# Second block's attention: scores and products on all 128 rows, q projected earlier, the output product in two halves of four blocks

## The chip, the cores and the metric

One core of a Trainium2 chip (trn2). The time is the device time of one execution of the whole program in microseconds; a kernel's time is the median of its runs.

## The reference

The program is two small models one after the other; the second one's layers are the diff attention (da), a gated FFN with a short convolution, the top-k sparse attention (dsa), and a second FFN. All of it is float32, with 528 tokens (16 meta tokens and 512 others) of width 1024. What the change touches is this:

```python
def diff_attention(h, w_qkv, lq1, lk1, lq2, lk2, subln, w_o, cos, sin, lambda_init):
    q, k, v = jnp.split(h @ w_qkv, 3, axis=-1)
    q = apply_rope(q.reshape(B, T, 8, 2, 64), cos, sin) * (64 ** -0.5)
    k = apply_rope(k.reshape(B, T, 8, 2, 64), cos, sin)
    v = v.reshape(B, T, 8, 128)
    lam = exp(sum(lq1 * lk1)) - exp(sum(lq2 * lk2)) + lambda_init
    s = einsum('bqhcd,bkhcd->bhcqk', q, k)            # two score maps per head pair
    p = softmax(where(k_pos <= q_pos, s, -inf))
    a = p[:, :, 0] - lam * p[:, :, 1]
    o = rms_norm(einsum('bhqk,bkhe->bqhe', a, v), subln) * (1.0 - lambda_init)
    return o.reshape(B, T, 1024) @ w_o

def dsa_attention(h, w_in, idx_k_norm, w_o, cos, sin, n_keys):
    q, k, v, qi, ki, wi = jnp.split(h @ w_in, DSA_SPLITS, axis=-1)   # 16 heads of 64, 8 index heads
    score = einsum('bqhk,bqh->bqk', relu(qi . ki) / 8, wi * 8 ** -0.5)
    score = where(causal, where(k_pos < 16, 1e30, score), -inf)
    keep the top min(256, n_keys // 4) keys of each query; softmax and product with v over these alone
    return o.reshape(B, T, 1024) @ w_o
```

The sliding-window attention (swa) of the first model has scores of 128 queries against 256 keys, and a first block that has only its own 128 keys.

## The kernel before, in words

Activations stand transposed in SBUF: 8 tiles of 128 features by 528 tokens. Every large product goes through `gemm` (line 366): each float32 operand is split into a high and a low part of type fp32r, and three products (high by high, high by low, low by high) of a 128x128 block are summed in PSUM, in pieces of 256, 258, 272 or 512 columns. Weights come from HBM in 294 chunks of 512 KB; ACT makes the high part (line 320) and DVE the low one (line 322). A scheduler sets the order of each engine's list at build time and interleaves the next product with the attention that is being worked on; the engines then run their lists in order and wait for one another on semaphores.

Both attentions go over eight pairs of heads. For each pair q and k are projected (`rope`, lines 770 to 774: a copy on ACT, a shuffle and products on DVE, one product on POOL, line 773, and a last sum on DVE, line 774). The queries are cut into five tiles: 16 meta tokens (i = 0) and four of 128 (i = 1 to 4); tile i reads the keys up to its own end (16, 144, 272, 400, 528).

- **Scores.** `pair_scores` picks one of two forms. `scores` (line 973), for i = 0 and 1, multiplies plain float32 q and k on the 64 rows of a head; PE runs such a product in two passes. `scores2` (line 1008), for i = 2 to 4, uses all 128 rows: `stack` (lines 987 and 988) lays the fp32r high part of a head's 64 rows on one half of the partitions and the low part on the other, `swapped` makes a copy k3 of the stacked k2 with the halves exchanged by two DMAs, and two products with k2 and k3 give the full-precision score.
- **Mask.** In da the causal mask is added on PE, by a bf16 product of the mask with the identity (lines 975 and 1010), whose weights are loaded just before. DVE then takes the maximum from PSUM (line 1111) and ACT the exponential from PSUM (line 1119). In dsa the mask with the top-k selection is a tile in SBUF that DVE adds while it takes the maximum and writes the scores to SBUF (line 1220).
- **Product with V.** `turn` transposes the weights on PE (lines 1029, 1033, 1036 and 1040) and copies them back, on DVE (line 1037) but for the last block. Then float32 products of two passes each: in da line 1134, with one of 16 rows for the first 16 keys and i of 128 rows; in dsa line 1244, the same, per head with 64 columns of output.
- **Output.** Da's results are normalised and transposed by `flip` (lines 1076 and 1080). `project_out` multiplies the heads 0 to 5 for all eight output blocks m, and after that the heads 6 and 7, each m followed by `next_h`, the preparation of the next layer's norm.

In da the pairs are a plain loop. In dsa the string ORDER tells when the pieces are emitted: S is a tile's scores and softmax, T its transposes and product, Gq and Gk the next pair's projections, X its stacks.

Of the kernel before, what the change touches and what calls it, by code (L numbers as in the profile page):

```python
# [16 lines left out]
P = 128  # L17
# [16 lines left out]
ORDER = "S0 T0 S1 T1 S2 T2 S3 T3 S4 T4 Gq Gk X".split()  # L34
# [94 lines left out]
def _out_blocks(w):  # L129
    return [_blocks(w[:768]), _blocks(w[768:])]  # L130
# [85 lines left out]
class _Kernel:  # L216
# [30 lines left out]
    def setup(self, gain):  # L247
# [8 lines left out]
        self.sq = self.pool(ctx, "sq", 2)  # L256
# [30 lines left out]
        for k in range(KB):  # L287
            self.square_in(self.x[k][:, lo:], k, 0, T, nc.vector)
# [83 lines left out]


# [174 lines left out]
    def mamba(self, g_next):  # L548
        nc, T = self.nc, SEQ
        tc = self.tc  # L550
        with ExitStack() as ctx:
            cp = self.pool(ctx, "mc", 1, reuse_waits="tile")
            yp = self.pool(ctx, "my", 8, reuse_waits="tile")
            wctx = ctx.enter_context(ExitStack())
# [224 lines left out]
    def project_v(self, vs, q, w, tiles, spread=False):  # L779

        nc = self.nc
        for i, t0, tn in tiles:
# [7 lines left out]
            for n, (k, a, b) in enumerate(steps):  # L790
                nc.tensor.matmul(ps[:tn, :256], a[k][:, t0:t0 + tn], w[k][b], start=n == 0, stop=n == 3 * KB - 1)  # L791
            nc.scalar.activation(vs[i][:tn, 256 * q:256 * q + 256], ps[:tn, :256], AF.Copy,
                                 scale=self.rt[:tn, i:i + 1])
# [37 lines left out]
    def swa(self, g_next):  # L831
# [3 lines left out]
        with ExitStack() as ctx:  # L835
# [29 lines left out]
            for b in range(KB):  # L865
# [6 lines left out]
                k = kr[b // 4]  # L872
                ks = k2[b // 4], k3[b // 4]
                q2 = self.stack(wp, q, "q2", P)
# [5 lines left out]
                for n0 in (0, 2):  # L880
                    for r in range(2):
                        rr = slice(64 * r, 64 * r + 64)
                        ps = self.ps("s")
                        for n in (n0, n0 + 1):
# [65 lines left out]
            wctx.close()  # L950
            self.out_halves(self.pool(ctx, "sx", 1, reuse_waits="tile"), OH[SF:], OL[SF:], ys,
# [10 lines left out]

    def scores(self, q, k, i, r, mask=None, lo=0):

        nc = self.nc
        t0, e = max(STARTS[i], lo), ENDS[i]
        tn = e - t0
        rr = slice(64 * r, 64 * r + 64)
        out = []
        for k0, k1 in ([(0, e)] if i < 4 else [(0, 272), (272, 528)]):  # L970
            ps = self.ps("s")
            last = mask is not None and k1 == e
            nc.tensor.matmul(ps[:tn, :k1 - k0], q[rr, t0:e], k[rr, k0:k1], start=True, stop=not last)  # L973
            if last:
                nc.tensor.matmul(ps[:tn, t0 - k0:e - k0], self.identb[:tn, :tn], mask[:tn, :tn], start=False,
                                 stop=True)
            out.append((ps[:tn, :k1 - k0], k0, k1))
        return out
# [20 lines left out]
    def scores2(self, q, ks, i, r, q0, mask=None):  # L999

        nc = self.nc
        t0, e = STARTS[i], ENDS[i]
        out = []
        for k0, k1 in ([(0, e)] if i < 4 else [(0, 272), (272, 528)]):
            ps = self.ps("s")[:, :k1 - k0]
            last = mask is not None and k1 == e
            for n, k in enumerate(ks):
                nc.tensor.matmul(ps, q[:, r, t0 - q0:e - q0], k[:, r, k0:k1], start=n == 0, stop=n == 1 and not last)  # L1008
            if last:
# [4 lines left out]
    def pair_scores(self, pool, q, k, mask=None, lo=0):  # L1014

        q0 = STARTS[2]
        q2 = self.stack(pool, q, "q2", q0)
# [26 lines left out]
    def da(self, g_next):  # L1044
        nc, T = self.nc, T2
        with ExitStack() as ctx:
# [37 lines left out]
            for h in range(8):  # L1084
# [15 lines left out]
                for i in range(5):  # L1100
# [39 lines left out]
                    if i == 2 and rest:  # L1140
                        flip(*rest)
# [320 lines left out]
```

## Time and profile before

| | before |
|---|---|
| median of 3 runs | 2182.44 us (2182.3 to 2183.26) |
| profiled execution | 2185.24 us |
| its span | 2183.5 us |
| PE | 2118.2 us busy, 97%, 15060 passes |
| DVE | 1533.0 us, 70% |
| ACT | 1004.8 us, 46% |
| POOL | 261.1 us, 12% |

The stages follow one another: mamba to about 450 us, swa to 678, da's start to 730, its eight pairs to 987, its output tail to 1026, the first FFN to 1411, dsa's index scores and top-k to 1527, its pairs to 1755, its tail to 1800, the second FFN to the end. A matmul's duration in the trace is modelled and overlaps the next one's, so costs on PE are read as steps from one start to the next.

### The profile page before, as it was taken

To read this page: it belongs to the slowest core of one execution; us is meant where nothing else is said; L and a number is where in the kernel's file an instruction comes from. 1 tells how busy PE (TensorE), PEld (TensorE's weight loads), DVE (VectorE), ACT (ScalarE), POOL (GpSimd) and SP (SyncE) were. 2 spreads that over 40 slices of the span, in tenths; PEclk is the share of its full clock that TensorE was granted. 3 is DMA by queue.
4 is the path that set the end of the run, shared out by engine and by line. 5 is a ranking of instruction groups with operands and counts; after the bars stand their busy time and mean duration, and the time that the engine had idled before them with its cause. 6 is when DMAs were issued, how large, how long until landed. Compare 5 with 4: busy or idle time off the path is not lost.

```text
span 2183.5 us, 38225 instructions
## 1 busy us (share of the span) xinstructions
PE 2118.2 (97%) x15060; PEld 1905.7 (87%) x15060; DVE 1533.0 (70%) x3318; ACT 1004.8 (46%) x1925; POOL 261.1 (12%) x380
## 2 busy tenths in 40 slices
PE   8999999999998999999999999999999999999998
PEld 6788888887777888889999999979788899999997
DVE  7786777787767677876673565499888866645653
ACT  6876555246774444544442333353444334423431
POOL 0221111141104111212000000121111020000001
PEclk9999999989998999999999999999999999999998
DMA  5434333314121321211323232312211223323331
GB/s 192 121 112 123 97 120 95 115 49 116 51 73 52 98 59 53 78 57 58 98 91 93 88 92 83 98 48 77 70 50 50 79 68 97 92 86 103 88 88 49
DMA packets 59570, 186.15 MB, mean 85 GB/s; under 512 B 8384, under 2 KB 12480, under 8 KB 59392
## 3 DMA queue, kind: packets, MB, share of 16 engines
q1 hardware_dynamic: 58240, 182.68, 27.9%
q8 instruction: 118, 1.93, 0.4%
q10 hardware_dynamic: 1152, 1.05, 0.1%
q14 instruction: 60, 0.49, 0.1%
HBM read 171.77 MB, written 2.23 MB: 80 GB/s over the span
## 4 chain that ended last, share of the span: by engine, by line
PE 79%; DVE 12%; issue 3%; ACT 2%; POOL 2%; DMA 1%; SPq 0%; POOLq 0%; DVEq 0%; ACTq 0%
PE ps_g L366 49%; PE ps_s L366 14%; PE ps_o L1244 2%; PE ps_s L1008 2%; PE ps_g L791 2%; PE ps_o L1134 2%; DVE wL L322 2%; DVE sel L1346 1%; DVE hL L397 1%; PE ps_t L1036 1%; POOL rs_r L412 1%; DVE m L1345 1%; PE ps_s L709 1%; PE ps_o L931 1%; PE ps_s L973 1%
## 5 line engine op out<-in xcount | busy, mean ns | idle before, releaser
L366 PE MATMUL ps_g<-hL,wH 128*128 128x256 f32 (+3 forms) x1912 | 610.1, 320 | 2.3 <-DVE hL L397 2.3
L366 PE MATMUL ps_g<-hH,wL 128*128 128x256 f32 (+3 forms) x1912 | 609.9, 319 | 1.7 <-DVE wL L322 1.7
L366 PE MATMUL ps_g<-hH,wH 128*128 128x256 f32 (+3 forms) x1912 | 607.4, 318 | 0.5 <-ACT hH L392 0.3
L320 ACT ACTIVATE wH<-raw 128x1024 fp32r<-128x1024 f32 x294 | 310.3, 1057 | 370.2 <-PE ps_g L366 217.8
L322 DVE TENSOR_TENSOR wL<-raw,wH 128x1024 fp32r<-128x1024 f32 x294 | 366.7, 1249 | 149.1 <-ACT wH L320 148.7
L366 PEld LDWEIGHTS ps_g<-hL,wH 128*128 128x128 f32 x1912 | 361.0, 189 | 29.5 <-issue 4.2
L366 PEld LDWEIGHTS ps_g<-hH,wL 128*128 128x128 f32 x1912 | 361.7, 189 | 27.4 <-issue 3.3
L366 PEld LDWEIGHTS ps_g<-hH,wH 128*128 128x128 f32 x1912 | 361.6, 189 | 26.0 <-issue 3.0
L366 PE MATMUL ps_s<-hH,wH 128*128 128x256 f32 (+5 forms) x608 | 178.2, 293 | 8.6 <-ACT hH L392 8.6
L366 PE MATMUL ps_s<-hH,wL 128*128 128x256 f32 (+5 forms) x608 | 178.2, 293 | 0.6 <-DVE wL L322 0.6
L366 PE MATMUL ps_s<-hL,wH 128*128 128x256 f32 (+5 forms) x608 | 177.7, 295 | 0.9 <-DVE hL L397 0.6
L383 POOL TENSOR_TENSOR acc<-acc,sq 128x512 f32<-128x512 f32 (+3 forms) x62 | 77.1, 1244 | 552.3 <-ACT sq L382 550.6
L1381 DVE SCALAR_TENSOR_TENSOR c<-u,prm,c 128x528 f32<-128x528 f32 (+1 forms) x176 | 132.9, 755 | 3.4 <-ACT c L1378 1.8
L773 POOL TENSOR_TENSOR rt<-rt,S 128x272 f32<-128x272 f32 (+3 forms) x80 | 81.3, 1018 | 408.7 <-DVE rt L771 313.3
L366 PEld LDWEIGHTS ps_s<-hH,wH 128*128 128x128 f32 (+2 forms) x608 | 115.8, 191 | 10.7 <-ACT hH L392 9.5
L366 PEld LDWEIGHTS ps_s<-hL,wH 128*128 128x128 f32 (+2 forms) x608 | 115.8, 192 | 4.4 <-DVE hL L397 3.2
L366 PEld LDWEIGHTS ps_s<-hH,wL 128*128 128x128 f32 (+2 forms) x608 | 116.3, 191 | 3.0 <-DVE wL L322 1.4
L366 PE MATMUL ps_g<-aH,wH 128*128 128x256 f32 (+1 forms) x418 | 118.5, 284 | 0.3
L366 PE MATMUL ps_g<-aH,wL 128*128 128x256 f32 (+1 forms) x418 | 118.7, 284 | 0.0
L366 PE MATMUL ps_g<-aL,wH 128*128 128x256 f32 (+1 forms) x418 | 118.6, 284 | 0.0
L798 ACT ACTIVATE aH<-sg 128x528 fp32r<-128x528 f32 (+1 forms) x44 | 28.1, 639 | 126.8 <-DVE sg L1386 126.8
L366 PE MATMUL ps_s<-aH,wH 128*128 128x256 f32 (+1 forms) x286 | 80.5, 282 | 0.4 <-ACT aH L798 0.4
(490 smaller groups left out, 4535.3 us busy)
## 6 DMA issues: line engine op xcount, KB each, us to landing
raw<-in_ws_dram SPq DMA_DIRECT2D x294, 512.0 KB, 3.7
k<-k SPq DMA_DIRECT2D x32, 264.0 KB, 3.6
m<-acs_d SPq DMA_DIRECT2D x32, 256.0 KB, 3.7
e<-eas_d SPq DMA_DIRECT2D x32, 96.0 KB, 2.8
x<-in_xT_dram SPq DMA_DIRECT2D x8, 256.0 KB, 5.2
xo<-in_xT_dram SPq DMA_DIRECT2D x8, 256.0 KB, 5.4
k<-k SPq DMA_DIRECT2D x4, 256.0 KB, 7.6
out_dram<-x SPq DMA_DIRECT2D x8, 128.0 KB, 1.7
```

What stands on the lines that cost most here:

```text
L320: nc.scalar.activation(H, self.raw, AF.Copy)
L322: nc.vector.tensor_tensor(L, self.raw, H.bitcast(F32), ALU.subtract)
L366: nc.tensor.matmul(ps[:M, :cn], w[k][a][:, :M], b[k][:, c0:c0 + cn], start=i == 0, stop=i == 3 * n - 1)
L383: (eng or nc.gpsimd).tensor_tensor(acc, acc, s[:, :cn], ALU.add)
L397: self.nc.vector.scalar_tensor_tensor(L, self.x[k][:, t0:t1], self.col(g, k), H.bitcast(F32), ALU.mult, ALU.subtract)
L773: nc.gpsimd.tensor_tensor(t, t, S[:, cc], ALU.mult)
L791: nc.tensor.matmul(ps[:tn, :256], a[k][:, t0:t0 + tn], w[k][b], start=n == 0, stop=n == 3 * KB - 1)
L798: nc.scalar.activation(H[:, cols], src, AF.Copy)
L1008: nc.tensor.matmul(ps, q[:, r, t0 - q0:e - q0], k[:, r, k0:k1], start=n == 0, stop=n == 1 and not last)
L1134: nc.tensor.matmul(dst, aT[j], vs[j][:ENDS[j] - STARTS[j], hc], start=j == 0, stop=j == i)
L1244: nc.tensor.matmul(dst, vs[j][:ENDS[j] - STARTS[j], hc], pT[r][j], start=j == 0, stop=j == i, skip_group_check=True)
L1381: nc.vector.scalar_tensor_tensor(c[:, lo:], u[:, t + lo:t + T2], self.col(fw, 3 * b + t), c[:, lo:], ALU.mult, ALU.add)
```

## The change

- All scores of the four 128-query tiles, of da, dsa, the index and swa's first block, now use the stacked 128-row form (`scores`, line 999 of the changed kernel).
- The masks on PE are gone: in da, too, DVE adds a mask tile (`wide`) while it takes the maximum, and ACT reads the scores from SBUF.
- The first 16 keys are no longer a 16-row product: in da the transposed block holds the first 128 keys and V's first tile is filled with zeros beyond 16; in dsa both heads' first 16 weights, padded to 64 each, are one 128-row product with `v0b` (line 1369) for the pair.
- The 16 meta queries of all eight pairs are gathered by copies on POOL (`meta_keep`) and worked on once, during the last two pairs (`meta_soft`, `meta_apply`).
- `turns_of` (line 1084) makes the transposes and copies four at a time, on ACT but for the second group.
- Both attentions run the new ORDER through `attend`. F projects k of the next pair, G projects q of the pair after the next; X, which stacks the next pair's q and k, stands after S4, and N ends a pair. q is written to `self.acc` and k to `self.rb`, one buffer each.
- The output product is cut after four heads. `out_first` (heads 0 to 3) fills F and G of the last two pairs, which have nothing to project; `out_last` multiplies heads 4 to 7 with `next_h`.
- The pool for squares is opened where it is used.

```diff
-ORDER = "S0 T0 S1 T1 S2 T2 S3 T3 S4 T4 Gq Gk X".split()
+ORDER = "S1 S2 T1 F S3 T2 S4 X T3 T4 N G".split()
...
 def _out_blocks(w):
-    return [_blocks(w[:768]), _blocks(w[768:])]
+    return [_blocks(w[:512]), _blocks(w[512:])]
...
-                            if n == 0:
-                                nc.tensor.matmul(ps[:, o1 - kn:o1], q[rr, :P], k[rr, :P], start=True, stop=True)
-                            else:
-                                for u in range(2):
-                                    nc.tensor.matmul(ps[:, o1 - kn:o1], q2[:, r, P * n - P:P * n],
-                                                     ks[u][:, r, k0:k0 + kn], start=u == 0, stop=u == 1)
+                            for u in range(2):
+                                nc.tensor.matmul(ps[:, o1 - kn:o1], q2[:, r, P * n:P * n + P],
+                                                 ks[u][:, r, k0:k0 + kn], start=u == 0, stop=u == 1)
...
-    def scores2(self, q, ks, i, r, q0, mask=None):
+    def scores(self, q, ks, i, r):
...
             for n, k in enumerate(ks):
-                nc.tensor.matmul(ps, q[:, r, t0 - q0:e - q0], k[:, r, k0:k1], start=n == 0, stop=n == 1 and not last)
-            if last:
-                nc.tensor.matmul(ps[:, t0 - k0:e - k0], self.identb, mask, start=False, stop=True)
+                nc.tensor.matmul(ps, q[:, r, t0:e], k[:, r, k0:k1], start=n == 0, stop=n == 1)
...
-        return lambda i, r: self.scores(q, k, i, r, mask, lo) if i < 2 else self.scores2(q2, ks, i, r, q0, mask)
+        return lambda i, r: self.scores(q2, ks, i, r)
...
+    def turns_of(self, pool, srcs, name, width):
+        nc = self.nc
+        t = pool.tile([P, width * P], F32, name=name)
+        for c0 in range(0, len(srcs), 4):
+            ps = self.ps("t")
+            n = min(4, len(srcs) - c0)
+            for j in range(n):
+                nc.tensor.transpose(ps[:, P * j:P * j + P], srcs[c0 + j], self.ident)
+            if c0 == 4:
+                nc.vector.tensor_copy(t[:, P * c0:P * (c0 + n)], ps[:, :P * n])
+            else:
+                nc.scalar.activation(t[:, P * c0:P * (c0 + n)], ps[:, :P * n], AF.Copy)
...
+                t = self.acc if nm == "q" else self.rb
+                self.rope(wp, self.gemm(self.wblocks(KB), self.hH, self.hL, self.cuts(T)), C, S, t)
+                self.meta_keep(h, nm, t)
...
+                        nc.vector.tensor_tensor_reduce(out=p[:, r, k0:k1], in0=pp, in1=wide[:, w0 + k0:w0 + k1],
+                                                       scale=1.0, scalar=-3.0e38, op0=ALU.add, op1=ALU.max,
+                                                       accum_out=mx[:, c:c + 1])
...
+                aT = self.turns_of(wp, [a[:, :P]] + [a[:, META + P * j:META + P * j + P] for j in range(i)], "aT", 5)
+                dst = po[:, P * (i - 1):P * i]
+                for j in range(i + 1):
+                    nc.tensor.matmul(dst, aT[j], vs[j][:, P * h:P * h + P], start=j == 0, stop=j == i)
...
+            def fill(h, op):
+                if op == "F":
+                    if h < 7:
+                        project(h + 1, "k")
+                    else:
+                        self.out_first(OH, OL, (2, 3, 4))
+                else:
+                    if h in (0, 2):
+                        self.project_v(vs, 2 + h // 2, self.vweights(), self.tok_tiles(T))
+                    if h < 6:
+                        project(h + 2, "q")
+                    else:
+                        self.out_first(OH, OL, (0, 1) if h == 6 else (5, 6, 7))
...
+    def out_first(self, H, L, ms, lo=0):
+        for m in ms:
+            for ps, c0, cn in self.gemm(self.wblocks(4), H[:4], L[:4], self.cuts(T2, lo)):
+                x = self.x[m][:, c0:c0 + cn]
+                self.nc.vector.tensor_tensor(x, ps, x, ALU.add)
...
+    def attend(self, fns, fill, meta):
+        for h in range(8):
+            po = self.ps("o")
+            for op in ORDER:
+                if op in ("F", "G"):
+                    fill(h, op)
+                    if h == 6 and op == "F":
+                        meta = meta()
+                elif op == "X":
+                    if h < 7:
+                        fns["X"](h + 1)
...
+                srcs = [pms[i % 2].rearrange("p r k -> p (r k)")] + [ps[i][:, r, META + P * j:META + P * j + P] for r in range(2)
+                                             for j in range(i)]
+                pT = self.turns_of(wp, srcs, "pT", 9)
+                nc.tensor.matmul(po[:, cc], v0[:, P * b:P * b + P], pT[0], start=True, stop=False,
+                                 skip_group_check=True)
```

How the order moves, in three places. First PE in da, at the scores of the tiles of 128 queries (L366 and L367 are the big products, ps_s the scores, identb the identity in bf16, v a tile of V). Before:

```order
L366 MATMUL ps_g<-hH_85,wL 128x272
L1008 MATMUL ps_s<-k_6852,q_6842 128x272
L1010 LDWEIGHTS identb
L1010 MATMUL ps_s<-maskb,identb 128x128
L1008 MATMUL ps_s<-k_6852,q_6842 128x272
L1010 LDWEIGHTS identb
L1010 MATMUL ps_s<-maskb,identb 128x128
L366 MATMUL ps_g<-hL_93,wH 128x272
```

The same place in the changed kernel:

```order
L367 MATMUL ps_g<-hL_93,wH 128x256
L999 MATMUL ps_s<-k_7160,q_7155 128x400
L999 MATMUL ps_s<-k_7165,q_7155 128x400
L999 MATMUL ps_s<-k_7160,q_7155 128x400
L999 MATMUL ps_s<-k_7165,q_7155 128x400
L1084 MATMUL ps_t<-ident,p 128x128 x3
L1179 MATMUL ps_t<-ident,on 128x128 x4
L999 MATMUL ps_s<-k_7160,q_7155 128x272
```

The mask products and their weight loads are gone, and the scores of both heads stand together.

Second, PE in dsa, at a product with V (two heads of a pair; v_14679 is V's tile of the first 16 keys before, v0b the padded one). Before:

```order
L366 MATMUL ps_g<-hL_95,wH 128x272
L1244 MATMUL ps_o<-pT,v_14679 64x128
L366 MATMUL ps_g<-hH_88,wH 128x272
L1244 MATMUL ps_o<-pT,v_14679 64x128
L1244 MATMUL ps_o<-pT,v_14680 64x128 x2
L366 MATMUL ps_g<-hH_88,wL 128x272
```

In the changed kernel:

```order
L367 MATMUL ps_g<-hH_79,wL 128x272
L1084 MATMUL ps_t<-ident,p 128x128
L1369 MATMUL ps_o<-pT,v0b 128x128
L1374 MATMUL ps_o<-pT,v_14450 64x128 x2
L1374 MATMUL ps_o<-pT,v_14451 64x128 x2
L1374 MATMUL ps_o<-pT,v_14452 64x128 x2
```

One 128-wide product takes the place of two 16-row ones with a big product between them.

Third, PE in da at the start of a pair, where the first scores stand behind a projection. Before, where the projection is that of the same pair's k:

```order
L366 MATMUL ps_g<-hH_88,wL 128x256
L366 MATMUL ps_g<-hL_96,wH 128x256
L973 MATMUL ps_s<-k,q 16x16
L975 LDWEIGHTS identb
L975 MATMUL ps_s<-maskb,identb 16x16
L973 MATMUL ps_s<-k,q 16x16
```

In the changed kernel, where it is that of q, for the pair after:

```order
L367 MATMUL ps_g<-hH_85,wH 128x256
L367 MATMUL ps_g<-hH_85,wL 128x256
L367 MATMUL ps_g<-hL_93,wH 128x256
L999 MATMUL ps_s<-k_7160,q_7155 128x144
L999 MATMUL ps_s<-k_7165,q_7155 128x144
L999 MATMUL ps_s<-k_7160,q_7155 128x144
```

The first score now reads the stacked q and k and the swapped k, and 48 products of another projection lie ahead of it.

## Rows read from the trace of the kernel before

**Rows 1.** The page, chain that ended last, by engine.
```profile
PE 79%; DVE 12%; issue 3%; ACT 2%; POOL 2%; DMA 1%; SPq 0%; POOLq 0%; DVEq 0%; ACTq 0%
```

**Rows 2.** Windows: stretch, length, busy time of each engine, granted clock, DMA share.
```profile
730.00:987.00 257.00, 245.87 (x1822) 215.58 (x1821) 199.08 (x609) 125.04 (x391) 48.58 (x86) 1.00 0.23 65
987.00:1026.00 39.00, 35.74 (x260) 35.04 (x259) 27.14 (x47) 15.56 (x23) 10.79 (x10) 0.90 0.27 78
...
1527.00:1755.00 228.00, 223.04 (x1753) 187.41 (x1754) 187.89 (x636) 101.39 (x272) 24.67 (x31) 0.99 0.24 65
1755.00:1800.00 45.00, 42.22 (x320) 40.56 (x317) 28.60 (x49) 16.88 (x24) 10.96 (x7) 0.92 0.22 64
```

**Rows 3.** Waits of PE, 730 to 987, then 1527 to 1755: total, times, longest.
```profile
PE ps_s L973 <- DVE k L774: 5.8, 3, 2.5
...
PE ps_s L973 <- DVE k L774: 4.4, 1, 4.4
```

**Rows 4.** Groups of PE by line, 730 to 987: count, busy, mean ns.
```profile
L366 PE MATMUL ps_g<-hL,wH 128*128 128x256 f32 (+1 forms) x233 | 68.1, 292 | 0.0
...
L791 PE MATMUL ps_g<-wL,hH 128*128 128x256 f32 (+1 forms) x80 | 21.1, 292 | 0.0
...
L366 PE MATMUL ps_g<-o1H,wH 128*128 128x272 f32 (+1 forms) x12 | 3.7, 307 | 0.0
```

**Rows 5.** The same view, 1527 to 1755.
```profile
L366 PE MATMUL ps_g<-hL,wH 128*128 128x256 f32 (+2 forms) x227 | 68.6, 302 | 0.0
```

**Rows 6.** Timeline of PE in da, tile i = 1 and a product of i = 4.
```profile
828.73 0.75 PE L791 MATMUL ps_g<-wH,hL 128*128 128x256 f32 x5
829.32 0.28 PE L791 MATMUL ps_g<-wH,hH 128*128 128x256 f32 x1
...
830.61 0.49 PE L1036 MATMUL ps_t<-ident,p 128*128 128x128 f32 x3
830.94 0.27 PE L1040 MATMUL ps_t<-ident,p 128*128 128x128 f32 x1
831.14 0.51 PE L973 MATMUL ps_s<-k,q 64*128 64x144 f32 x2
...
832.22 0.36 PE L791 MATMUL ps_g<-wL,hH 128*128 128x256 f32 x1
832.51 1.57 PE L1134 MATMUL ps_o<-v,aT 16*128 16x128 f32 x10
834.01 0.18 PE L1029 MATMUL ps_t<-ident,p 16*16 16x16 f32 x1
```

**Rows 7.** Timeline of PE in da, the sixteen-query tile's scores.
```profile
868.31 0.21 PE L973 MATMUL ps_s<-k,q 64*16 64x16 f32 x2 [2.46 <-DVE k L774]
...
868.79 0.39 PE L366 MATMUL ps_g<-hL,wH 128*128 128x272 f32 x1
```

**Rows 8.** Timeline of PE in da, a mask of tile i = 2.
```profile
835.97 0.23 PE L1010 MATMUL ps_s<-maskb,identb 128*128 128x128 bf16 x1
836.00 0.36 PE L791 MATMUL ps_g<-wL,hH 128*128 128x256 f32 x1
836.21 0.51 PE L791 MATMUL ps_g<-wH,hL 128*128 128x256 f32 x3
```

**Rows 9.** Timeline of PE in dsa, a product with V of tile i = 4.
```profile
1565.28 0.43 PE L1244 MATMUL ps_o<-pT,v 16*64 16x128 f32 x2
1565.63 0.39 PE L366 MATMUL ps_g<-hH,wL 128*128 128x256 f32 x1
1565.85 0.28 PE L366 MATMUL ps_g<-hL,wH 128*128 128x256 f32 x1
...
1566.54 1.45 PE L1244 MATMUL ps_o<-pT,v 16*64 16x128 f32 x18
1567.92 0.19 PE L1029 MATMUL ps_t<-ident,p 2*16 2x2 f32 x2
```

**Rows 10.** The page, DMA issues: size, median us to landing.
```profile
k<-k SPq DMA_DIRECT2D x32, 264.0 KB, 3.6
```

More of the change, by code (lines that the diff above doesn't have):

```diff
@@ L286, in setup @@
         self.wchunk()
-        for k in range(KB):
-            self.square_in(self.x[k][:, lo:], k, 0, T, nc.vector)
+        with ExitStack() as sctx:
+            self.squares(sctx)
+            for k in range(KB):
+                self.square_in(self.x[k][:, lo:], k, 0, T, nc.vector)
         if first:
@@ L371, in gemm1, with squares @@
         return next(iter(list(self.gemm(w, H, L, self.cuts(T), M, spread))))[0]
+    def squares(self, ctx):
+        self.sq = self.pool(ctx, "sq", 2, reuse_waits="tile")
     def square_in(self, src, k, c0, cn, eng=None, acc=None):
@@ L777, in vweights, with project_v @@
         return [self.wget(2) for k in range(KB)]
-    def project_v(self, vs, q, w, tiles, spread=False):
+    def project_v(self, vs, q, w, tiles, spread=False, meta=None):
         nc = self.nc
@@ L1037, in turn @@
-        nc.vector.tensor_copy(t[:, :P + n1 * P], ps[:, :P + n1 * P])
-        if i == 4:
-            ps = self.ps("t")
-            nc.tensor.transpose(ps[:, :P], a[:, META + 3 * P:], self.ident)
-            nc.scalar.activation(t[:, 4 * P:], ps[:, :P], AF.Copy)
-        return [t[:META, :tn]] + [t[:, P + P * j:2 * P + P * j] for j in range(i)]
+        self.qm = pool.tile([P, 8, 2, META], F32, name="qm")
+        nc.gpsimd.memset(self.qm, 0.0)
+        self.km = pool.tile([P, 8, META], F32, name="km")
@@ L1070, in da @@
                     nc.vector.tensor_tensor(S[:, c0:c0 + cn], S[:, c0:c0 + cn], self.rb[:, c0:c0 + cn], ALU.mult)
-            OH, OL = [], []
-            def flip(H, L, o0, on):
-                pt = self.ps("t")
-                nc.tensor.transpose(pt[:, :META], o0, self.ident[:META, :META])
-                self.split(H, L, pt[:, :META], slice(0, META), gs)
+            OH = [cp.tile([P, T2], F32R, name=f"o{h}H") for h in range(8)]
+            OL = [cp.tile([P, T2], F32R, name=f"o{h}L") for h in range(8)]
@@ L1078, in flip @@
+            def flip(h, on):
                 pt = self.ps("t")
@@ new lines, in da, with apply_flip, start, finish @@
+            rest = []
+            def apply_flip(h, i, po):
+                apply(h, i, po)
+                if i == 2 and rest:
+                    flip(*rest.pop())
+            def start(h, i, po):
+                if i == 1:
+                    sums[h] = [self.sm.tile([P, 8], F32, name=nm) for nm in ("dens", "ssq")]
+                    for t in sums[h]:
+                        nc.gpsimd.memset(t, 1.0)
+                soft(h, i)
+            def finish(h, po):
+                dens, ssq = sums[h]
@@ L1249, in dsa, with finish, fill @@
+            def finish(b, po):
+                self.split(OH[b], OL[b], po, slice(META, T2))
+            def fill(b, op):
+                if b < 7 and op == "F":
+                    project(b + 1, "k")
+                elif b < 6:
+                    project(b + 2, "q")
+                else:
+                    self.out_first(OH, OL, (2, 3, 4) if op == "F" else (0, 1) if b == 6 else (5, 6, 7), lo)
             project(0, "q")
```

383 lines of the change are left out of this document (207 added, 176 removed).

## The prediction

> **What bounds the kernel now.** I read the share of busy time and the chain first, then the windows by stage, then the timeline inside the stages that change. The chain lies on PE for 79% of the span and on DVE for 12% [rows 1]. The change is almost wholly inside two stages: the attention of the first layer (da, 730 to 987 us) and of the second (dsa, 1527 to 1755 us), each with its output tail behind it. In these windows PE is busy 245.87 of 257 us and 223.04 of 228 us [rows 2], at a granted clock of 1.00 and 0.99 (2.4 GHz): PE has no slack to hide in, and DVE has (199.08 and 187.89 us). So each PE step removed there should count, as long as DVE, next at 77% and 82%, can follow.
>
> How much of PE's time is attention? In da the window holds 233 + 233 + 232 projection products, 240 of V, and 18 groups of 12 or 11 output products, 213 in all [rows 4]. One 256-column product costs 0.118 us: five from 828.73 to 829.32 [rows 6]; a 272-column one I take in proportion, 0.126, the mean 0.122. So 911 x 0.122 + 240 x 0.118 = 139 us are big products, 11 us are idle, and 257 - 139 - 11 = **107 us are attention forms**, 13.4 a pair. In dsa there are 3 x 227 projections and 159 output products (681 in all by [rows 5]; the 159 are counted in the program): 840 x 0.12 = 101 us, 5 us idle, so 228 - 101 - 5 = **122 us**, 15.2 a pair.
>
> **What the new forms cost.** A pair has four query tiles, whose scores in full rows are 4 narrow products (144 columns), 4 of 272, 4 of 400, and 4 of 272 with 4 of 256. The 400-column step is 0.184 in proportion. That is 4 x 0.126 + 4 x 0.184 + 4 x 0.126 + 4 x 0.118 = 2.2 us, and the 4 narrow ones. The trace of before has no full-row product of this type under 256 columns. Below, the price in proportion to columns is 0.065; above, twice the 256-column step, 0.24, as an operand type that takes two passes shows. I take 0.11, the pace of other 128-column steps with a new weight each (three transposes from 830.61 to 830.94 [rows 6]): 0.45. Then for da 14 transposes x 0.11 = 1.5, 14 products with V in two passes each, 28 x 0.11 = 3.1, four flips 0.44: 7.7 us. Every entry of such a block between the big products costs some 0.09 more (below), at about 12 places a pair, 1.1 us; the sum is 8.8, and one sixteen-row query tile for all pairs (some 90 small steps and three waits of a chain, not above 3 us a stage) adds 0.4: 9.2. For dsa there are 24 transposes, 2.6 us, and in each of four tiles one two-pass product at full rows (0.22) and 4i half-width passes, 40 in all at half of 0.11: 0.9 + 2.2; with scores 2.65, entries 1.5, meta 0.4 it is 10.3. So PE would save (13.4 - 9.2) x 8 = **33 us in da** and (15.2 - 10.3) x 8 = **39 us in dsa**.
>
> **Does the timeline say the same?** It shows which forms carry it.
> - Masks on PE. A mask step takes 0.03 and makes the product behind it 0.21 instead of 0.118 [rows 8]: 0.12 each, six a pair, 6 us over da. DVE now adds the mask while it takes the maximum, an instruction it ran anyway.
> - First query tile of 128. Both heads' 64-row scores with masks take 831.14 to 832.22, 1.08 us, then the next step 0.29 instead of 0.118 [rows 6]. New 0.45, so 0.7 to 0.8 a pair: 6 us.
> - Sixteen-key products with V. The ten passes from 832.51 to 834.01 take 1.50 [rows 6]; ten at 0.11 are 1.1. With the slower step behind, 0.35 to 0.4, four a pair: 12 us. In dsa the pair of 16-row passes takes 0.35 and the big product behind it 0.22, and each of the two heads does it, the second in a run of 18 passes of 1.38, of which 16 should take 0.9 [rows 9]. That is about 1.2 us a tile against 0.22 and an entry: 0.8, 32 tiles: 26 us.
> - The sixteen-query tile. Scores and masks take 868.31 to 868.79 [rows 7], and its transpose, product and flip with their entries about 1 us more: 1.5 a pair, less 0.4: 9 us in each stage.
> These give 33 in da and about 40 in dsa (26, 9, and 5 for the first tile), so I take 33 and **37**. SWA's first block (16 pairs of heads, 64-row two-pass scores into full rows) and the index scores are the same exchange on 32 and 16 products; by the saving per product above, 0.1 us, that is 5 us together.
>
> A rule of the Trainium skill speaks against the edit: "TensorEngine Tiling (Array Packing)", Theoretical Speedup, says that a contraction of 64 or less run as row tiles gains up to 2x, and the kernel gives these tiles up. By it the first query tile would lose, some 0.45 a pair, 7 us over both stages. The trace speaks against it for this order: two heads' 64-row passes, each needing two for full precision, took 0.54 us a head, mask included, against 0.22 estimated for a head's two full-row products. The same page's Key Properties say that a change of the tiling mode drains the engine; the step behind each foreign form (0.21 for 0.118) agrees.
>
> **Tails.** Before, six of eight blocks are multiplied first and the last two come with the norm: twelve products, 1.46 us per output block, against DVE's two adds, square and split. PE is idle 3.3 of 39 and 2.8 of 45 us there, at a mean clock of 0.90 and 0.92 [rows 2], which is worth 3.9 and 3.6 more (part of it ran at 1.2 GHz). With four blocks at the end PE has 24 products, 2.9 us, and DVE fits below. The gain lies between 0 and 7.2 + 6.4; since the chain behind the last block (norm, transposes) stays, I take 6 and 5, **11 us**. The first half, out_first, fills the last two pairs, which otherwise have no projection to interleave.
>
> **Waits.** S0 waited for k's rope three times in da, 5.8 us, at most 2.5, and once in dsa, 4.4 [rows 3]. Now a whole projection of q (48 products, 5.9 us) stands between k and the first score of the next pair. In dsa I take 3 of the 4.4 as gained: the top-k chain on DVE stands ahead of the ropes and is unchanged. In da I take no gain: DVE's share rises. It loses the transposes' copies and small steps, some 20 us, while the window loses 33: 179 of 224 is 80% (dsa, with 28 less, 160 of 188, 85%). ACT takes the copies (125 + 8 of 224) and is not near. The maxima now write the scores to memory and PE's two score buffers wait for them as in dsa before. So the 11 us of idle time in da stay, in other places, and in dsa I add 5. POOL takes 1 to 3 small copies per projection for the meta tile, behind the rope's own step: beside PE's work. The two swap DMAs (3.6 us [rows 10]) are issued in X, with T3, T4 and the projection G, over 8 us, ahead of their reader: nothing. The scoped pool for squares and the wider first block of V (products of 128 instead of 16 rows at the same step) cost nothing that PE sees.
>
> **Sum.** The profiled execution took 2185.2 us, 2.8 above the median of the three runs. 2185.2 - 33 - 37 - 5 - 11 - 3 + 5 = 2101, and on the median's scale **2098 us**.
>
> **Rivals.**
> - A, narrow products are dear. If a 144- or 128-column full-row product costs 0.24, 112 of them (32 in each of four places, 16 in the index) lose 0.13 each, 15 us: 2113. Nothing in the trace shows one. 0.13.
> - B, slower: the swap becomes exposed. k2 and k3 are now read by a pair's first score, while before the first two tiles read q and k themselves. If DVE and ACT reach X so late that the 3.6 us of the DMA and the 2.5 us after the rope [rows 3, 10] lie bare, each of 15 pair starts loses 6.1, 92 us: 2190. It decides from 5.6 us a pair on. Against it: over 8 us of PE work lie between, and DVE has 15 to 20% left. 0.05.
> - C, waits go as well: with q one and a half pairs ahead, PE loses the idle time of da and dsa too, 11 + 5 + 5 less: 2077. For it: each wait in rows 3 is one for k's rope, which is now covered. 0.22.
> - D, DVE sets the pace: at 80 to 85% with one score buffer per head, PE waits 1.5 us more in each of 16 pairs: 2122. For it: DVE carries 12% of the chain already. 0.12.
>
> **How the numbers follow.** The forecast has 0.48. Its own range, from the narrow price (0.065 to 0.24 is -5 to +15), the tails (+11 to -3) and forms (10 either way), is 2085 to 2115. The range takes in C's and D's spread: **2066 to 2130**. A measurement here can tell 0.2%, 4.4 us, from no change. Only B and the worst of D reach there: faster 0.93, same 0.02, slower 0.05.
>
> **What would show it.** Right: PE's busy time near 2040, the two attention stages 33 to 38 us shorter each, no bf16 products, the step behind a score 0.118, tails at a clock near 1. Wrong: narrow scores at 0.2 or more (A), PE waiting for k2's or k3's DMA at a pair's start (B), or long waits for DVE's maxima (D).

## The result and the profile after

The changed kernel takes 2165.92 us (median of 4 runs, 2165.13 to 2166.37) against 2182.54 us before: a ratio of 0.992, 95% interval 0.9906 to 0.9935, 0.8% faster. The forecast was 2098. The direction held; of the 84 us that were forecast 17 came.

The page's first lines of the changed kernel show it roughly. PE's busy time fell by 42 us, where 78 were forecast (2118.2 to near 2040); its share fell too, so PE now stands idle more.

```profile
span 2162.7 us, 37624 instructions
PE 2076.2 (96%) x14812; PEld 1894.4 (88%) x14812; DVE 1488.3 (69%) x3215; ACT 1023.6 (47%) x1874; POOL 275.5 (13%) x433
```

The windows (columns as in [rows 2]) of the changed kernel's two attention stages and tails. The stretches are the same work but for the edges.

```profile
742.00:987.00 245.00, 224.04 (x1719) 210.48 (x1718) 178.34 (x592) 128.52 (x340) 52.20 (x102) 0.97 0.25 68
987.00:1024.00 37.00, 35.88 (x294) 35.53 (x293) 23.28 (x43) 17.69 (x24) 11.87 (x11) 1.00 0.29 86
...
1520.00:1740.00 220.00, 209.86 (x1648) 186.60 (x1649) 175.23 (x571) 113.49 (x270) 34.53 (x60) 0.97 0.25 71
1740.00:1785.00 45.00, 43.96 (x355) 43.51 (x354) 26.41 (x51) 19.91 (x27) 11.04 (x7) 0.96 0.26 80
```

The tails answer to the forecast: idle 1.1 and 1.0 us instead of 3.3 and 2.8, a clock of 1.00 and 0.96 instead of 0.90 and 0.92 [rows 2]. The attention stages don't: PE's idle time rose from 11 to 21 us in da and from 5 to 10 in dsa, and the clock fell to 0.97 in both.

Whole pairs of dsa tell the forms apart from the edges: four before (388 big products) and three of the changed kernel (288).

```profile
1558.00:1664.90 106.90, 106.68 (x847) 89.19 (x846) 91.20 (x318) 51.26 (x140) 13.57 (x17) 1.00 0.21 56
```

```profile
1582.50:1654.10 71.60, 70.19 (x566) 62.22 (x564) 61.07 (x202) 40.68 (x96) 12.02 (x21) 1.00 0.24 68
```

A pair of dsa went from 26.7 to 23.9 us, 2.9 less, with idle 0.1 and 0.5; eight give 23. For da, where the projections are spread otherwise over the pairs, the prediction's own sum serves: length, less idle time, less the big products. In the window of the changed kernel 1151 big products at 0.122 us make 140, so 245 - 21 - 140 = 84 us are attention forms instead of 107. In the run without the chain for the meta queries (the first one below) the same window has 1269 big products, 155 us, and 16 us of idle time: 74 us of forms, some 4 a pair less than before, near what was forecast. So the forms came in da, and in part in dsa, and the time was lost again elsewhere. Where the largest part went, the timeline of PE shows in pair 6 of da:

```profile
931.83 0.32 PE L1045 MATMUL ps_t<-km,qm 128*32 128x16 f32 x16
932.08 0.55 PE L1084 MATMUL ps_t<-ident,p 128*128 128x128 f32 x3
...
936.39 0.50 PE L999 MATMUL ps_s<-k,q 128*128 128x256 f32 x2 [1.16 <-DVE mx L1150]
936.72 0.29 PE L1063 MATMUL ps_t<-ident,pm 128*128 128x128 f32 x1
938.84 1.86 PE L1072 MATMUL ps_t<-mv,v 128*128 128x16 f32 x8 [1.82 <-DVE mv L1187]
940.54 0.45 PE L1084 MATMUL ps_t<-ident,p 128*128 128x128 f32 x1
940.79 1.73 PE L1072 MATMUL ps_t<-mv,v 128*128 128x16 f32 x8
942.35 0.88 PE L1084 MATMUL ps_t<-ident,p 128*128 128x128 f32 x3
943.92 2.07 PE L1171 MATMUL ps_o<-v,aT 128*128 128x128 f32 x8 [0.69 <-ACT aT L1088]
945.79 0.42 PE L1197 MATMUL ps_t<-ones,msq 128*128 128x1 f32 x2
```

Lines 1045, 1063, 1072 and 1197 are the chain for the sixteen meta queries. From 931 to 952 us there is not one big product: F of pair 6 (k of pair 7) is done, and G, the first part of the output product, reads the meta columns of heads 0 to 3, so it stands behind the chain. PE waits at each link: from 931 to 940 us it is busy for 5.7 of 9 us, and from 940.79 to 950 us the granted clock is 0.50 (1.2 GHz):

```profile
931.00:940.00 9.00, 5.70 (x50) 4.69 (x48) 8.25 (x31) 6.88 (x18) 1.98 (x2) 0.91 0.21 58
940.79:950.00 9.21, 6.93 (x30) 5.93 (x30) 4.58 (x16) 3.28 (x9) 0.75 (x2) 0.50 0.23 59
```

There the small steps cost double: the eight passes (four products of 16 columns, two passes each) from 940.79 to 942.35 take 0.195 us each. The same eight passes take 0.10 each at a clock of 1.00, in the run below with the chain in two halves (its lines 1068 and 1080):

```profile
864.50 0.96 PE L1068 MATMUL ps_t<-mv,v 128*128 128x16 f32 x8
865.31 0.63 PE L1080 MATMUL ps_t<-ident,p 128*128 128x128 f32 x4
```

### The profile page after: what moved, and what is told of

It is laid out like the page before. It is cut to its first block, busy times and chain, and to the rows that moved or that the text cites. A ratio compares the mean times of both kernels' runs of the same rounds, so it can differ in the third digit from the quotient of the medians.

```text
span 2162.7 us, 37624 instructions
## 1 busy us (share of the span) xinstructions
PE 2076.2 (96%) x14812; PEld 1894.4 (88%) x14812; DVE 1488.3 (69%) x3215; ACT 1023.6 (47%) x1874; POOL 275.5 (13%) x433
## 5 line engine op out<-in xcount | busy, mean ns | idle before, releaser
L367 PE MATMUL ps_g<-hL,wH 128*128 128x256 f32 (+3 forms) x1912 | 606.7, 318 | 2.5 <-DVE hL L401 2.4
L367 PE MATMUL ps_g<-hH,wH 128*128 128x256 f32 (+3 forms) x1912 | 607.1, 318 | 1.4 <-ACT kr L775 1.1
L367 PE MATMUL ps_g<-hH,wL 128*128 128x256 f32 (+3 forms) x1912 | 606.5, 317 | 1.8 <-DVE wL L323 1.8
L367 PEld LDWEIGHTS ps_g<-hL,wH 128*128 128x128 f32 x1912 | 361.4, 189 | 26.9 <-DVE hL L401 3.9
L367 PEld LDWEIGHTS ps_g<-hH,wL 128*128 128x128 f32 x1912 | 362.3, 189 | 25.1 <-DVE wL L323 2.4
L367 PEld LDWEIGHTS ps_g<-hH,wH 128*128 128x128 f32 x1912 | 362.0, 189 | 24.1 <-ACT kr L775 1.2
L367 PE MATMUL ps_s<-hH,wH 128*128 128x256 f32 (+5 forms) x608 | 177.6, 292 | 8.0 <-ACT hH L396 8.0
L367 PE MATMUL ps_s<-hH,wL 128*128 128x256 f32 (+5 forms) x608 | 177.4, 292 | 0.6 <-DVE wL L323 0.6
L367 PE MATMUL ps_s<-hL,wH 128*128 128x256 f32 (+5 forms) x608 | 176.9, 294 | 0.7 <-DVE hL L401 0.6
L367 PEld LDWEIGHTS ps_s<-hH,wH 128*128 128x128 f32 (+2 forms) x608 | 114.8, 189 | 10.4 <-ACT hH L396 9.1
L367 PE MATMUL ps_g<-aH,wH 128*128 128x256 f32 (+1 forms) x418 | 118.3, 283 | 0.3 <-ACT aH L810 0.2
L367 PEld LDWEIGHTS ps_s<-hL,wH 128*128 128x128 f32 (+2 forms) x608 | 114.3, 189 | 4.8 <-DVE hL L401 3.7
L367 PE MATMUL ps_g<-aL,wH 128*128 128x256 f32 (+1 forms) x418 | 118.2, 283 | 0.0
L367 PE MATMUL ps_g<-aH,wL 128*128 128x256 f32 (+1 forms) x418 | 118.0, 282 | 0.0
L367 PEld LDWEIGHTS ps_s<-hH,wL 128*128 128x128 f32 (+2 forms) x608 | 115.1, 189 | 3.3 <-DVE wL L323 1.4
L999 PE MATMUL ps_s<-k,q 128*128 128x272 f32 (+3 forms) x400 | 91.1, 323 | 13.6 <-DVE q L979 4.4
```

The lines of the kernel that those rows point to most:

```text
L367: nc.tensor.matmul(ps[:M, :cn], w[k][a][:, :M], b[k][:, c0:c0 + cn], start=i == 0, stop=i == 3 * n - 1)
L999: nc.tensor.matmul(ps, q[:, r, t0:e], k[:, r, k0:k1], start=n == 0, stop=n == 1)
```

## The experiments

Times of each run stand beside the kernel before on the same chip (2182.5 to 2183.3 us in all batches); 2166 is the changed kernel, which was timed in the first batch only. In its profiled execution the 200th big product, in mamba, which no edit touches, starts at 69.0 us; in the 15 other kernels' it starts at 65.6 to 67.8. So 1 to 3 us of a difference from its trace are not the edit's, and prices of a few us are taken between the same big products of two traces ("by place").

**The meta chain left out.** In both attentions the generator of the chain only writes zeros:

```diff
             def metas():
-                t = yield from self.meta_soft(wp)
...
+                for t in OH + OL:
+                    nc.gpsimd.memset(t[:, :META].bitcast(F32), 0.0)
+                yield
```

> Leaves out the chain of the sixteen meta queries (their outputs are set to zero); all else is the changed kernel. Theory W (the new forms cost what they should, but idle time and a lower clock give the gain back, most of it where the meta chain stands bare in pair 6): 20 to 26 us faster than the changed kernel's 2166, so 2140 to 2146, with no drop of the clock near 938 and 1696 us. Rival F (the new forms are simply dearer on PE than estimated): only the chain's own small steps go, 3 us a stage, so 2160.

Measured: 2139.72 us (2139.16 to 2141.02), 26 us faster. The windows from 930 to 987 and from 1690 to 1740 us, first of the changed kernel, then without the chain:

```profile
930.00:987.00 57.00, 51.21 (x377) 48.13 (x377) 37.57 (x132) 25.55 (x71) 6.48 (x11) 0.88 0.17 47
1690.00:1740.00 50.00, 46.37 (x359) 40.52 (x358) 32.58 (x114) 21.57 (x56) 0.73 (x1) 0.90 0.16 45
```

```profile
930.00:987.00 57.00, 55.44 (x445) 53.70 (x444) 40.48 (x116) 28.90 (x65) 10.23 (x11) 1.00 0.26 75
...
1690.00:1740.00 50.00, 49.91 (x421) 47.68 (x420) 33.45 (x87) 23.13 (x43) 8.71 (x6) 1.00 0.25 75
```

The clock drop goes with the chain. By place it is 12.1 us in da and 10.0 in dsa, 22 together; the other 4 lie where the edit changes nothing, 2.2 of them in mamba's start. Theory W held for the chain: its own steps were put at 3 us a stage, the other 16 us are waits and the clock. Whether the forms cost what they should, the other half of W, this run doesn't decide.

**The chain in two halves.** `meta_soft` and `meta_apply` take a half g and work on heads 4g to 4g + 3:

```diff
-                    if h == 6 and op == "F":
-                        meta = meta()
+                    if h == 3 and op == "F":
+                        cur = meta(0)
...
+                    if h == 7 and op == "S1":
+                        cur = meta(1)
```

> The changed kernel with the meta chain in two halves: heads 0 to 3 in pair 3, heads 4 to 7 in pair 7, both where independent projections or output products are at hand. Theory W (the chain's price of 26 us is waiting and the clock, because in pair 6 all that could fill depends on it): 18 to 22 us faster than the changed kernel, 2144 to 2148, clock near 1 at both places. Rival (its many small steps are the price): as the changed kernel or slower by 2 to 6, 2166 to 2172.

Measured: 2152.38 us (2151.2 to 2152.76), 13.5 us faster. The windows:

```profile
742.00:987.00 245.00, 227.84 (x1790) 213.73 (x1790) 185.48 (x615) 132.34 (x347) 56.25 (x104) 1.00 0.25 72
...
1515.00:1730.00 215.00, 208.03 (x1667) 185.42 (x1667) 175.03 (x579) 112.97 (x269) 33.69 (x60) 0.99 0.26 75
```

The clock is back at 1.00 and 0.99. The gain is short of the 18 to 22 expected; by place it is 6.5 us in da and 5.6 in dsa, 12 of the chain's 22. The chain's transposes and the steps of its norm run twice now, and some waits remain. The cause holds, the size was too large.

**The first block of the sliding window as before.** The 64-row branch for n == 0 is put back into the changed kernel:

```diff
+                            if n == 0:
+                                nc.tensor.matmul(ps[:, o1 - kn:o1], q[rr, :P], k[rr, :P], start=True, stop=True)
```

> The changed kernel with the sliding-window attention's first block back in 64-row two-pass products. The stages before da ended 8.4 us later in the changed kernel than before, and da's start lost 4.6 more. Theory S1 (the new form of the first block, which waits for the stacked q, is the cause): 5 to 9 us faster than the changed kernel, 2157 to 2161. Rival S2 (the scoped pool for squares is the cause): within 2 us of 2166. By price alone, with no waits: 3 us slower, 2169.

Measured: 2159.82 us (2157.31 to 2161.31), 6 us faster. By place 2.9 us of it fall in swa, between the 1800th and the 2400th big product, which is back at its length before; 2.5 lie in mamba's start. So the change to full rows there cost some 3 us where 3 were counted as a gain. The waits of PE from 500 to 690 us, in the changed kernel and then with the old form, show part of it: two waits for ACT to empty PSUM are gone (the wait for wL in the second is that of da's start, which lies past 690 in the first).

```profile
PE ps_s L899 <- DVE q L979: 1.7, 3, 1.1
PE ps_g L367 <- ACT q L775: 1.1, 1, 1.1
PE ps_g L367 <- ACT k L956: 1.1, 1, 1.1
```

```profile
PE ps_s L797 <- DVE wL L323: 5.2, 1, 5.2
PE ps_s L901 <- DVE q L779: 1.4, 2, 1.1
```

**Only the scoped pool for squares, in the kernel before.**

```diff
-        self.sq = self.pool(ctx, "sq", 2)
...
+    def squares(self, ctx):
+        self.sq = self.pool(ctx, "sq", 2, reuse_waits="tile")
```

with `self.squares(ctx)` in each stage, as in the change.

> The kernel before, with one change: the pool for squares opened where it is used. Theory S1: nothing, 2182.5 within 1.5 us. Rival S2 (it moves loads and products in the first stages): 4 to 9 us slower, 2187 to 2191.

Measured: 2189.46 us (2186.87 to 2191.95), ratio to before 1.0024 (1.0014 to 1.0034): 6 us slower, so S2 holds beside S1. In the profiled runs 3.7 us of it fall between the 1000th and the 1800th big product, in mamba's second half and the start of swa, where PE now waits 1.1 us for a copy that stands late in ACT's list (line 775), and 4.2 us in da, where the only difference to see is a granted clock of 0.91 instead of 1.00 from 780 to 840 us, behind the same wait of 2.4 us for k's rope; 1.8 come back between. Of the 3.7 the kernels with the new pool show 2.1 to 3.1 us too, against those with the old one. So the pool's own price is some 3 us. Why the clock fell in da isn't settled.

**Only the cut of the output product, in the kernel before.**

```diff
-    return [_blocks(w[:768]), _blocks(w[768:])]
+    return [_blocks(w[:512]), _blocks(w[512:])]
...
-        for k0, k1 in ((0, 6), (6, 8)):
+        for k0, k1 in ((0, 4), (4, 8)):
```

> The kernel before, with one change: the output product cut 4+4 instead of 6+2, its first half still behind the last pair. Theory T (the two output tails are worth what was forecast, and by the cut alone): 10 to 14 us faster than before, 2169 to 2173. Rival: the gain needs the first half to fill the last pairs: within 3 us of 2182.5.

Measured: 2175.63 us (2173.9 to 2177.05), ratio 0.9964 (0.9951 to 0.9977): 7.7 us faster. The cut alone does it; the filling of the last pairs isn't needed for that. That is short of the 10 to 14 expected, and of the term of 11. By place the two tails are 5.7 and 5.6 us shorter, 11 as forecast; 2.9 us are lost between them, at dsa's start, where behind the same wait of 1.2 us for the norm (line 447) the granted clock is 0.83 instead of 1.00. Windows of the same work, before and in this run:

```profile
1405.00:1425.00 20.00, 18.24 (x121) 15.38 (x120) 9.66 (x25) 3.82 (x5) 2.35 (x3) 1.00 0.33 107
```

```profile
1399.00:1419.00 20.00, 18.20 (x106) 15.17 (x104) 7.88 (x21) 3.81 (x5) 2.61 (x3) 0.83 0.32 107
```

Some 2 to 3 us are lost at the same products in the runs with the chain in halves above, and with G early and N late below, and none in the changed kernel; why the clock falls there in some and not in others isn't settled.

**The order.** Twice the dense order, first in the changed kernel:

```diff
-ORDER = "S1 S2 T1 F S3 T2 S4 X T3 T4 N G".split()
+ORDER = "S1 T1 S2 T2 S3 T3 S4 T4 N F X G".split()
```

> The changed kernel with the emission order S1 T1 S2 T2 S3 T3 S4 T4 N F X G: each product directly behind its scores, k of the next pair and then q of the pair after next at the pair's end; the meta chain stands whole behind F of pair 6. Theory O (the new order is worth something, since it sets scores two tiles ahead of their product): 10 to 30 us slower than the changed kernel, 2176 to 2196, with more waits for the softmax's last step. Rival (the scheduler fills the gaps either way): within 4 us of 2166.

Measured: 2179.09 us (2175.66 to 2180.87), 13 us slower. By place 11.7 us of it fall in da's pair 6, where the edit also makes the chain run whole, ahead of the pair's G; dsa as a whole is 5 us longer, and elsewhere it is about even. So this run alone doesn't tell an order's worth. G ahead of T3 and T4:

> The changed kernel with q's projection G emitted before T3 and T4, and in pair 6 the meta chain run to its end before it. Theory L: big products stand where PE waited for the softmax of the tiles 3 and 4, so da loses up to 10 us of waits, 2156 to 2162. Rival: the swap of k is then uncovered at the next pair's start, one to three us a pair, 2175 to 2200.

Measured: 2168.64 us (2165.87 to 2169.1), 3 us slower; no wait of the size expected by either went or came. By place da's pairs 0 to 5 are even with the changed kernel within 2 us, pair 6 loses 7, where here too the chain runs to its end ahead of G, and dsa gains 3.

**Less work for DVE.** The changed kernel without da's combination of the two maps:

```diff
-                nc.vector.scalar_tensor_tensor(p[:, 0, :e], p[:, 1, :e], den[:, 1:2], p[:, 0, :e], ALU.mult, ALU.add)
```

> The changed kernel; da leaves out the combination of the two score maps (a = p0 + c p1, about 20 us of DVE over da), so the product uses the first map alone. Theory L (PE's waits for this step, 9.9 us in da, are DVE coming late in its own order): 8 to 10 us faster than the changed kernel, 2156 to 2158. Rival F (PE is the bound and its forms are dear): 0 to 2 us, 2164 to 2166.

Measured: 2171.43 us (2170.07 to 2172.08), 5.5 us slower, a miss for both. In da DVE has 156.69 us to do instead of 178.34. By place da is 8 us longer; PE's idle time in the window from 742 to 987 us is up by 1.4 us only, and the granted clock is 0.93 instead of 0.97. PE's waits change their place. The waits of PE from 742 to 987 us, of the changed kernel and then of this one:

```profile
PE ps_t L1084 <- DVE p L1162: 9.9, 12, 1.2
PE ps_o L1171 <- ACT aT L1088: 3.6, 12, 0.7
PE ps_s L999 <- DMA k<-k: 2.5, 1, 2.5
PE ps_s L999 <- DVE mx L1150: 2.1, 3, 1.2
```

```profile
PE ps_s L999 <- DVE mx L1150: 14.7, 8, 3.1
PE ps_s L999 <- DMA k<-k: 1.7, 1, 1.7
```

DVE's list of this kernel shows what stands ahead of the maximum that PE waits for, at 872 us:

```profile
872.78 0.17 DVE L417 TENSOR_TENSOR rs_t<-ssq,rs_r 128x5 f32<-128x5 f32 x1 [1.72 <-POOL rs_r L416]
872.98 0.17 DVE L418 TENSOR_TENSOR rs_t<-rs_t,rs_r 128x5 f32<-128x5 f32 x1
...
875.71 0.42 DVE L779 TENSOR_TENSOR acc<-acc,rt 128x256 f32<-128x256 f32 x1 [0.62 <-POOL rt L778]
876.05 0.30 DVE L1150 CUSTOM_DVE_ANT_0 p<-ps_s,wide 128x144 f32<-128x144 f32 x1
...
876.41 0.77 PE L999 MATMUL ps_s<-k,q 128*128 128x272 f32 x4 [3.09 <-DVE mx L1150]
```

The norm of the pair before (lines 417 to 420) waits for a power on POOL, and the next pair's first maximum is queued behind it on DVE; PE's two score buffers wait for that maximum. So here the place in DVE's list sets the wait, not DVE's load. That was tried in the changed kernel, where a part of PE's wait for p should go with it:

```diff
-                rs = self.sm.tile([P, 8], F32, name="ors")
-                self.rsqrt(rs[:, :5], ssq[:, :5])
+                rs = ssq
```

> The changed kernel; da leaves out the reciprocal square root of each pair's norm (one POOL power and four DVE steps a pair; the unrooted sums are used instead). Theory H (DVE stands 0.9 us or more behind POOL's power, with the next pair's softmax queued behind it, and PE waits for that softmax): da loses 5 to 9 us, 2157 to 2161. Rival (PE's waits there come from somewhere else in DVE's list): within 2 us, 2164 to 2168.

Measured: 2159.52 us (2157.18 to 2159.89), 6.4 us faster; by place da's pairs are 4 us shorter, in steps of 1.1 us at the head of four pairs, and 2.3 lie in mamba's start. The wait for p fell from 9.9 to 6.2:

```profile
PE ps_t L1084 <- DVE p L1162: 6.2, 12, 1.2
```

Theory H's cause held; its size, 5 to 9, was too large, and the rest of the wait has another place. To keep the norm and move it behind S1 and S2 of the next pair:

```diff
+                    if op == "T1":
+                        if late:
+                            fns["N"](*late)
+                        po = self.ps("o")
```

> The changed kernel with N, the end of a pair (in da its norm chain, in dsa its split), emitted behind S1 and S2 of the next pair. Theory H: the softmax of the next pair no longer stands behind POOL's power, 4 to 9 us faster, 2157 to 2162. Rival: the sum of V's products is held longer and the next pair's first product waits for its buffer, 3 to 15 us slower, 2169 to 2181.

Measured: 2163.96 us (2160.97 to 2166.77), 2 us faster; in its trace 2.8 us are gained in mamba's start and lost again at dsa's start, where the clock falls, and da is unchanged. The scheduler sets DVE's list by its own rules, and where it put the chain this line doesn't tell. Open.

**Several things undone.** The halves of the chain, the old first block, and the pool for squares of the first two layers kept by itself:

```diff
+        self.sqctx = ctx.enter_context(ExitStack())
+        self.sq = self.pool(self.sqctx, "sq", 2)
```

> The changed kernel with three things altered: the meta chain in two halves, the sliding-window attention's first block in its old 64-row form, and the pool for squares of the first two layers kept apart from the other pools, as before. If the three prices measured one by one add up (13.5, 6, and 6 us, of which the last two may overlap): 8 to 12 us faster than the meta halves alone, 2140 to 2145. Rival (the two early ones are one and the same wait): 2146 to 2150.

Measured: 2142.09 us (2141.23 to 2142.98), ratio to before 0.9813. That is within what was expected from the sum of the prices. With the dense order on top:

> The kernel with three things undone (2142), with the emission order S1 T1 S2 T2 S3 T3 S4 T4 N F X G. Theory O (the new order is worth 13 us by itself, as the dense order alone showed): 2152 to 2160. Rival M (those 13 us were the meta chain, which stood whole behind F in pair 6; elsewhere the order is worth nothing or costs 3 to 5 us): 2136 to 2144.

Measured: 2142.6 us (2141.21 to 2146.28). The same within the spread of 5 us: rival M held. Once the chain has work beside it, the new order, with k projected in a pair's middle and scores two tiles ahead of their product, shows no gain over the dense one, with k projected at the pair's end.

**dsa's forms.** The last two start from the kernel with three things undone.

```diff
-                nc.tensor.matmul(po[:, cc], v0[:, P * b:P * b + P], pT[0], start=True, stop=False,
-                                 skip_group_check=True)
+                for r in range(2):
+                    nc.tensor.matmul(po[64 * r:64 * r + 64, cc], v0[:, P * b + 64 * r:P * b + 64 * r + 64], pT[0],
+                                     start=True, stop=False, skip_group_check=True)
```

> The kernel with three things undone (2142), with the 128-column product of the first 16 keys in dsa written as two 64-column products, so that a tile's product with V has one shape throughout. Theory D (dsa's forms were sized too low because a change between 128 and 64 columns costs 0.1 us, and it happens 32 times inside the products): 3 us faster, 2138 to 2140, and the step behind the product 0.1 instead of 0.2. Rival (the changes lie beside waits and cost nothing): within 1 us of 2142.

Measured: 2140.2 us (2137.75 to 2141.67), 2 us faster, but between the same big products dsa's pairs 1 to 6 are not shorter (0.1 us); 1.5 of the 2 lie at dsa's start. The edit removes no change of shape but moves it to the front of the product: inside it the step of 0.2 is gone, and the entry takes 0.21 to 0.26 instead of 0.15 to 0.17. So it can't tell; my expectation was at fault. With N late as well:

> The same, with N emitted behind S1 and S2 of the next pair. Theory H (DVE behind POOL's power holds the next softmax; the chain left out was worth 6.4 us): 2 to 5 us faster than the halves alone, 2134 to 2138. Rival (the order only shifts the place of the waits): within 1.5 us of the halves alone.

Measured: 2140.07 us (2136.8 to 2140.98): no gain. These two are the fastest of the kernels here that leave nothing out, 2% below before (0.9799, 0.9784 to 0.9815, for the first).

## Why the prediction was wrong

The direction, PE as the engine that sets the time, the price of da's forms and the tails were right; the size failed, in da by what stands around the forms, in dsa by the forms too.

- **Da's forms: right.** Without the chain a pair was to need 13.4 - 8.8 = 4.6 us less of PE, and some 4 came (107 to 74 us for eight). The step that failed is "the 11 us of idle time in da stay": it is 21 with the chain and 16 without. For part of it the place in DVE's list, not its share, made the wait: taking 22 us of work from DVE lengthened the run, taking the wait for POOL out of its list shortened da's pairs by 4. Rival D named DVE, but by its load; that part of it fell.
- **Dsa's forms: too low.** 39 us (taken as 37) were forecast, about 23 came. The step that failed is the entry, counted at 0.09 a block. A product of tile i = 2 in the changed kernel's timeline of PE:

```profile
1571.96 0.28 PE L367 MATMUL ps_g<-hL,wH 128*128 128x258 f32 x1
1572.24 0.49 PE L1369 MATMUL ps_o<-pT,v0b 128*128 128x128 f32 x2
1572.66 0.88 PE L1374 MATMUL ps_o<-pT,v 128*64 128x128 f32 x8
1573.47 0.51 PE L999 MATMUL ps_s<-k,q 128*128 128x256 f32 x2
```

  The first product's two passes take 0.42 instead of 0.22, and the eight behind 0.81, where eight at 0.055 are 0.44. This tile is one of the dear ones; over all 32 tiles of the trace, by medians, the step into the first product is 0.14 and its first pass 0.21, the change from 128 to 64 columns 0.205 (in each of 25 looked at) against 0.11 without, the step out 0.20 and the next big product 0.22 against 0.12. Above the bare passes that is 0.46 us a tile, 15 us, and ten tiles that are cut in two by big products cost 0.37 more each: 18.6 us, where 32 entries of 0.09, 2.9 us, were counted. The 15.7 more are the 16 that are missing. The Trainium skill, "TensorEngine Tiling (Array Packing)", Key Properties, says that a change of the tiling mode drains the engine; the 0.205 for 0.11 agrees. The 0.21 behind a mask [rows 8], which the prediction counted with it, does not bear on it: a mask is 128*128, and its 0.03 and the 0.21 behind together are no more than 0.11 and 0.12. All this is read from the trace; no run took the changes away.
- **The sixteen-query tile: the largest miss.** "Not above 3 us a stage" was the price of its steps. It measured 22 us in the two stages (12.1 and 10.0), because pair 6 has nothing independent left: the order that the prediction quotes ("fills the last two pairs, which otherwise have no projection") put the filler behind the chain. That was to be read in the code: `out_first` reads the columns that the chain writes.
- **Edits costed at nothing.** The scoped pool for squares, "nothing that PE sees", cost 6 us by the medians and some 3 by place, in stages that the change doesn't otherwise touch. The sliding window's first block cost some 3 where it should have gained 3. And da's start, not in the sum at all, is 5 us longer: in the changed kernel PE waits there for the sum of the norm (line 438), where the kernel before has one wait of 1.9.

```profile
713.94 0.98 PE L438 MATMUL ps_t<-ones,acc 128*128 128x1 f32 x4 [4.65 <-DVE lam L1107]
```

  Fewer V products stand ahead of it in PE's list now, 120 instead of 136; that they are the reason no run tries.
- **Tails: right**, 11 us by place, though the run with the cut alone was only 7.7 faster.
- **Rival A fell.** Two narrow full-row scores of the changed kernel take 0.18 us together, 0.09 each, below the 0.11 taken, and far from 0.24:

```profile
894.96 0.34 PE L999 MATMUL ps_s<-k,q 128*128 128x144 f32 x2
895.14 0.33 PE L367 MATMUL ps_g<-hH,wH 128*128 128x272 f32 x1
```

- **Rival B fell:** the swap shows once, 2.5 us at da's first pair.
- **Rival C fell:** the waits of da for k's rope did go, but others took their place, and idle time doubled. In dsa the 4.4 us for k's rope [rows 3] became 3.2 for the stacked k, 1.2 gained of the 3 taken:

```profile
PE ps_s L999 <- DVE k L979: 3.2, 2, 2.8
```

- The rule on row tiles of the Trainium skill, "TensorEngine Tiling (Array Packing)", Theoretical Speedup, would have made da's first query tile lose. Da's pairs fell by some 4 us of PE; no run here tries that tile alone.

In sum, by place, from the two profiled executions (spans of 2183.5 and 2162.7 us, 20.8 less): mamba's start +2.4, the rest of mamba and swa +5.3, da's start +5.2, da's pairs and tail -19.5, the first FFN +0.5, dsa -13.3, the rest -1.5. Without the chain da's pairs and tail would be at -31.6 and dsa at -23.3, against forecasts of 39 (33 and 6) and 40 (37, 5 and 3, less 5).

## What to carry to other kernels

When small serial work is gathered from many places into one, its price is the idle time at the place where it is put: look which independent work is left there, and whether the filler reads the chain's result. Where PE waits for an engine that isn't full, read what stands ahead in that engine's list, above all a step that waits for a third engine. Cost a change of form from a whole block in the trace, with the steps into and out of it, not from the pace in the middle of a run.

## What was not expected of the hardware

A float32 product of 128 rows behind an fp32r one costs a slower step without any change of the array's shape: where a product with V in da follows a big product without a wait (nine cases in the changed kernel), the step into it is 0.26 us and its first pass 0.21, against 0.12 and 0.11 inside each kind. And the clock answered to gaps of a few microseconds: in the 57 us behind 930 us it was granted at 0.88 in the mean with the chain's waits and at 1.00 without them. It doesn't follow from one wait alone: behind the wait of 1.2 us at dsa's start it was 1.00 before and 0.83 in the run with the cut output product.
